# A chunked delta-rule recurrence with state and values stacked on the contraction rows

## Chip, core and metric

The kernel runs on one core of a Trainium2 chip. Its time is the device time of one execution in microseconds (us). The engines work side by side, each with an instruction queue of its own: TensorE (PE for its products, PEld for the weight loads that stand ahead of them), VectorE (DVE), ScalarE (ACT), GpSimd (POOL) and SyncE (SP), which issues most DMAs.

## What is computed

One layer of a decoder trunk on 512 positions of width 2048, all in float32. The input is normalised and multiplied with a wide matrix; part of the columns goes to 16 recurrent heads of width 64, part to a causal pooling branch. Both are gated, joined, multiplied with an output matrix, and a gated embedding and a last normalisation follow. What the change touches is the recurrence of the heads:

```python
def step(S, inp):
    r_t, w_t, k_t, v_t, kk_t, a_t = inp
    sa = jnp.einsum('bhvk,bhk->bhv', S, -kk_t)
    S = (S * w_t[:, :, None, :]
         + sa[..., None] * (kk_t * a_t)[:, :, None, :]
         + v_t[..., None] * k_t[:, :, None, :])
    y_t = jnp.einsum('bhvk,bhk->bhv', S, r_t)
    return S, y_t
```

## The kernel before

The 512 positions are cut into 8 chunks of 64 and the 16 heads into 8 pairs (index `j`), since two heads of width 64 fill 128 partitions. Inside a chunk the recurrence is solved in closed form. With the state S at the chunk's start, the scaled keys and queries (`ar`: the k-side and the r-side; `bk`: the kk-side and the k-side), four masked 64 x 64 products of `bk` with `ar` are needed (`scores`, line L623 masks them on DVE), one of which has to be inverted as a unit triangular matrix (`invert` does its 32 x 32 diagonal blocks on DVE, after a trip through memory by the tensors `nd` and `xd`; the rest of `gather` completes it on TensorE with `pq` and `px`).

Then `recur` goes through the chunks, one head pair at a time. In each chunk there are three hops, each a TensorE product, then a short operation of another engine that the next product needs:

1. `py`: both sides of `ar` times the block-diagonal state `sbd` of the two heads (128 x 128, so one product serves both heads). DVE adds `mv`, the masked product with the values (made for all chunks beforehand by the block `pmv` in `gather`), into `zs` (L787). The first chunk of a head pair has no such hop.
2. `pu`: the inverse `x1` times `zs`. ACT copies the two diagonal blocks into `uv` (L797), where u and v of a chunk lie one above the other.
3. `ps` (`pss` in the code): `bkn`, the transposed `bk`, times `uv`. DVE scales it by the chunk's decay and adds the decayed old state `s0p` (made by POOL), one operation a head (L809); this is the next `sbd`.

After every fourth chunk eight products of half width (`py<-uv,mt` in the profile) add the part of y that comes from inside the chunks, and ACT copies y out (`ysb`).

The hops have nothing to do with each other's engines, so TensorE would stand idle between them. It does not, since the large products of the layer (the input matrix in blocks of 128 columns `zk`, `zr`, `zv`, `zg`, `zb`, and the embedding) are cut into steps and put between the hops. `pump(n)` issues about n of them; they come in threes (`mm3`, L157), because each float32 matrix is split into a high and a low float32r part. What is issued too many is carried over to the next call. `HC` gives the number after each of the three hops, `H1` to `H5`, `HX` those at places in `gather` and around `scores`, and `pump_to` rounds the position after the scores to a unit of `sum(HC)` or to `HC[2]` within it. During this part all TensorE instructions stay in the order of the program. The other engines' instructions are ordered by a scheduler at compile time, with the hand-overs of the hops (`tc.high_priority`) ahead of other work, and the steps of `invert` for the next head pair tied behind the last hand-over (`lead`).

PSUM tiles come from pools: `psM` has three (`m`), `psY` two (`y`), `psS` one, `psA` two for the large products.

Of the kernel before, what the change touches and what calls it, by code (L numbers as in the profile page):

```python
# [9 lines left out]
F32 = mybir.dt.float32  # L10
# [5 lines left out]
P = 128  # L16
T = 512
# [17 lines left out]
def trunk_kernel(ctx: ExitStack, tc: tile.TileContext, x, p, norm_g, w_in, mu, w0, w_up, a0, a_up,  # L35
# [56 lines left out]
    msk = cst.tile([P, 3, C], F32, name="msk")  # L92
    nc.gpsimd.memset(msk, 1.0)
    for h in range(2):
        rows = slice(64 * h, 64 * h + 64)
        for i in range(3):
            keep_if(msk[rows, i, :], [[1, C]], ALU.is_ge, -(i % 2), -1)
# [261 lines left out]
    sbd = [rw.tile([P, P], F32, name=f"sbd{i}") for i in range(2)]  # L359
    zsp = [rw.tile([P, P], F32, name=f"zs{i}") for i in range(2)]  # L360
# [4 lines left out]
    for t_ in sbd + zsp:  # L365
        nc.gpsimd.memset(t_, 0.0)
# [150 lines left out]
    H1, H2, H3, H4, H5, HE = 6, 12, 20, 8, 13, 40  # L517
# [59 lines left out]
    def prepare(j):  # L577
# [3 lines left out]
        if j + 1 < NJ:  # L581
# [3 lines left out]
        ar = rw.tile([P, NCH // 2, 4, C], F32, name=f"ar{j}", tag="ar", bufs=2)  # L585
        bk = rw.tile([P, NCH // 2, 4, C], F32, name=f"bk{j}", tag="bk")
        k4 = kk.rearrange("p (q c t) -> p q c t", c=2, t=C)
        pw4 = pw.rearrange("p (q c) t -> p q c t", c=2)
        i4 = ipw.rearrange("p (q c) t -> p q c t", c=2)
# [4 lines left out]
        nc.vector.tensor_tensor(ar[:, :, 0::3, :], r_.rearrange("p (q c t) -> p q c t", c=2, t=C),  # L594
                                pw4[:, :, :, 1:C + 1], ALU.mult)
        nc.vector.tensor_tensor(bk[:, :, 0::3, :], kp.rearrange("p (q c t) -> p q c t", c=2, t=C), i4, ALU.mult)
        nc.vector.scalar_tensor_tensor(ar[:, :, 1:3, :], k_.rearrange("p (q c t) -> p q c t", c=2, t=C), dp(89, j),
                                       pw4[:, :, :, 0:C], ALU.mult, ALU.mult)
        nc.vector.tensor_tensor(kk, kk, tha, ALU.mult)
        nc.vector.tensor_tensor(bk[:, :, 1:3, :], k4, i4, ALU.mult)  # L600
# [7 lines left out]
    def scores(j):  # L608
        ar, bk, v_ = (st_[j][n_] for n_ in ("ar", "bk", "v_"))
        kph, kpl = st_[j].pop("kp")  # L610

        mt = rw.tile([P, 2, 8, 2, C], F32, name=f"mt{j}", tag="mt", bufs=2)
        pm = [[psM.tile([P, T], F32, name=f"pm{j}_{par}0", tag="m"),
               psY.tile([P, T], F32, name=f"pm{j}_{par}1", tag="y")] for par in range(2)]
        for par in range(2):
            for q in range(4):
                for h in range(2):
                    rows = slice(64 * h, 64 * h + 64)
                    mm(pm[par][h][:, q * P:(q + 1) * P], bk[rows, q, 2 * par:2 * par + 2, :],
                       ar[rows, q, 2 * par:2 * par + 2, :], start=True, stop=True)  # L620
        for par in range(2):
            for h in range(2):
                nc.vector.tensor_tensor(mt[:, par, h::2, :, :],  # L623
                                        pm[par][h].rearrange("p (u a t) -> p u a t", u=4, a=2),
                                        msk[:, par:par + 2, :].unsqueeze(1).to_broadcast([P, 4, 2, C]), ALU.mult)


# [7 lines left out]
        for par in range(2):  # L635
            pb = 64 * (1 - par)
            for b in range(2):
                rows = slice(pb + 32 * b, pb + 32 * b + 32)
                nc.sync.dma_start(out=nd[par, b].rearrange("u r c -> r u c"),
                                  in_=mt[rows, par, :, 1 - par, 32 * b:32 * b + 32])  # L640
# [6 lines left out]
        st_[j].update(mt=mt, nb=nb, bv=bv)  # L647


    def invert(j):  # L650
# [16 lines left out]
        x1 = rw.tile([P, 8, C], F32, name=f"x1{j}", tag="x1", bufs=2)  # L667
        nc.gpsimd.memset(x1, 0.0)
        for par in range(2):
            pb = 64 * (1 - par)  # L670
            for b in range(2):
                nc.sync.dma_start(out=x1[pb + 32 * b:pb + 32 * b + 32, :, 32 * b:32 * b + 32],
                                  in_=xd[par, b].rearrange("u i q c -> (i q) u c"))

# [3 lines left out]
    def gather(j):  # L678
        d = st_[j]
        bk, v_, mt = d.pop("bk"), d.pop("v_"), d["mt"]  # L680
# [4 lines left out]
        uv = rw.tile([P, NCH, P], F32, name=f"uv{j}", tag="uv")  # L685
        ps = psY.tile([P, T], F32, name=f"pv{j}", tag="y")
# [3 lines left out]
        nc.scalar.copy(uv[0:64, 0::2, :], pv[0:64])  # L690
        nc.scalar.copy(uv[64:128, 1::2, :], pv[64:128])


        bkn = rw.tile([P, NCH, P], F32, name=f"bkn{j}", tag="bkn")
        for hf in range(2):
            ps = psM.tile([P, T], F32, name=f"pbk{j}_{hf}", tag="m")
            for i in range(4):
                ch = 4 * hf + i
                tr(ps[:, i * P:(i + 1) * P], bk[:, ch // 2, 2 * (ch % 2):2 * (ch % 2) + 2, :], ident)
            nc.scalar.copy(bkn[:, 4 * hf:4 * hf + 4, :], ps.rearrange("p (c n) -> p c n", n=P))  # L700

        pump(H4)

        ps = psM.tile([P, 8, C], F32, name=f"pmv{j}", tag="m")
        for u in range(8):
            for par in range(2):
                pb, kb = 64 * (1 - par), 64 * par
                h = u % 2
                mm(ps[pb:pb + 64, u, :], mt[kb:kb + 64, par, u, 1 - par, :],
                   uv[kb:kb + 64, 2 * (u // 2) + par, 64 * h:64 * h + 64], start=True, stop=True)  # L710
        mv = rw.tile([P, 4, P], F32, name=f"mv{j}", tag="mv")
        nc.scalar.copy(zsp[0][64:128, :].rearrange("p (h t) -> p h t", h=2), ps[64:128, 0:2, :])
        nc.scalar.copy(mv.rearrange("p q (h t) -> p (q h) t", h=2), ps)

        d.update(uv=uv, bkn=bkn, mv=mv)
# [7 lines left out]
        x1 = d["x1"]  # L723

        def units(fn):
            for u in range(8):
                for par in range(2):
                    fn(u, par, 64 * (1 - par))
# [3 lines left out]
        with tc.issue_after(late[0].ins):  # L732
            for pb in (0, 64):
                yt = nc.vector.transpose(y1[pb:pb + 32], x1[pb:pb + 32, :, 0:32])
# [4 lines left out]
        units(lambda u, par, pb: mm(ps3[pb + 32:pb + 64, u, :],  # L739
                                                  mt[pb:pb + 32, par, u, 1 - par, 32:64],  # L740
                                                  y1[pb:pb + 32, u, :], start=True, stop=True,
                                                  tile_position=(pb, pb + 32)))
        q2t = rw.tile([P, 8, 32], F32, name=f"q2{j}", tag="xw")
        for pb in (0, 64):
# [3 lines left out]
        units(lambda u, par, pb: mm(ps4[pb:pb + 32, u, :], q2t[pb + 32:pb + 64, u, :],  # L748
                                                  x1[pb + 32:pb + 64, u, 32:64], start=True, stop=True,
                                                  tile_position=(pb + 32, pb)))  # L750
        for pb in (0, 64):
            nc.scalar.copy(x1[pb:pb + 32, :, 32:64], ps4[pb:pb + 32])
# [3 lines left out]
    def recur(j, work, between):  # L756
        d = st_.pop(j)
        pw, ar, mt, bv, uv, bkn, mv, x1 = (d[n_] for n_ in ("pw", "ar", "mt", "bv", "uv", "bkn", "mv", "x1"))
# [5 lines left out]
        def step():  # L764
            hop[0] += 1
            if hop[0] > HS:
# [6 lines left out]
        py = None  # L773
        for ch in range(NCH):
            par, q = ch % 2, ch // 2
            pb = 64 * (1 - par)
            cur, nxt = sbd[ch % 2], sbd[(ch + 1) % 2]
            pcc = pw[:, ch, C:C + 1]
            sl = slice((ch % 4) * P, (ch % 4 + 1) * P)
            if ch % 4 == 0:  # L780
                py = psY.tile([P, T], F32, name=f"py{j}_{ch}", tag="y")
            zs = zsp[par]
            if ch > 0:
                mm(py[:, sl], ar[:, q, 2 * par:2 * par + 2, :], cur, start=ch in (1, 4), stop=True,
                                 skip_group_check=True)
                with tc.high_priority(offset=HP):
                    lead[0] = nc.vector.tensor_tensor(zs[pb:pb + 64], py[pb:pb + 64, sl], mv[pb:pb + 64, q, :],  # L787
                                                      ALU.add)
                step()
                pump(HC1)  # L790

            psu = psS.tile([P, T], F32, name=f"pu{j}_{ch}", tag="s")
            mm(psu[:, 0:P], x1[:, 2 * q:2 * q + 2, :], zs, start=True, stop=True)
            for h in range(2):
                hc = slice(64 * h, 64 * h + 64)
                with tc.high_priority(offset=HP):
                    nc.scalar.copy(uv[pb:pb + 64, ch, hc], psu[hc, hc])  # L797
            step()
            pump(HC2)
            if ch < NCH - 1:  # L800
                pss = psS.tile([P, T], F32, name=f"ps{j}_{ch}", tag="s")
                mm(pss[:, 0:P], bkn[:, ch, :], uv[:, ch, :], start=True, stop=True)
                for h in range(2):
                    hc = slice(64 * h, 64 * h + 64)
# [376 lines left out]
```

## Time and profile before

| | |
|---|---|
| median of 3 runs | 1100.12 us (1098.21 to 1101.85) |
| span of the profiled execution | 1095.9 us |
| own time of the profiled execution | not on the page, which gives the span alone |
| busy: PE, PEld, DVE, ACT, POOL | 98%, 80%, 65%, 41%, 7% |
| instructions on TensorE (products) | 6060 |
| granted TensorE clock, mean | 0.998 |

A row of a group has the line, engine, operation, the tile written and those read, the array's rows and columns in use, the shape, the count, then the busy time and the mean of one, then the idle time of the engine ahead of it with what ended it. A timeline row has start and duration in us. PE's durations are modelled and overlap, so what a product costs TensorE is read from the distance of starts.

### The profile page before, as it was taken

Reading aid. Unit: us, or ns where it says so; the run is one execution under the profiler, and the core shown is the slowest. Engines: PE = TensorE matmul, PEld = TensorE weight load, DVE = VectorE, ACT = ScalarE, POOL = GpSimd, SP = SyncE. Lnnn points to the kernel's source line nnn. Section 1 sums busy time; section 2 is a strip of 40 time slices with the busy share of each in tenths; the row PEclk is TensorE's granted clock in tenths of the full one; section 3 lists DMA queues with packets and bytes.
Section 4 is the critical chain, followed back from the end, with each engine's and each line's share of the span. In section 5 each row is a group of like instructions: output and inputs, shape, how many; then the busy total and the mean of one; then the engine's idle time right before and its main releaser. Section 6 shows DMA issues by size and latency. Waiting matters only on the chain.

```text
span 1095.9 us, 17196 instructions
## 1 busy us (share of the span) xinstructions
PE 1070.8 (98%) x6060; PEld 877.6 (80%) x6060; DVE 708.2 (65%) x1835; ACT 448.3 (41%) x917; POOL 76.9 (7%) x180
## 2 busy tenths in 40 slices
PE   5999999999999999999999999999999999999996
PEld 4888878887788888788878788888888888888885
DVE  6687867878688679678886956454433424445366
ACT  7633535345335335353343344543222222233337
POOL 2100110110110110100101101000000000000000
PEclk9999999999999999999999999999999999999999
DMA  7433433332423333333334242775534438455534
GB/s 233 116 96 97 111 92 84 96 100 73 120 82 105 104 92 89 96 82 93 91 94 119 79 138 93 232 233 169 172 124 136 167 99 244 137 189 137 181 106 154
DMA packets 178486, 138.56 MB, mean 126 GB/s; under 512 B 34678, under 2 KB 139743, under 8 KB 178399
## 3 DMA queue, kind: packets, MB, share of 16 engines
q1 hardware_dynamic: 157694, 103.89, 32.1%
q10 hardware_dynamic: 20704, 33.56, 9.8%
q8 instruction: 48, 0.79, 0.3%
q14 instruction: 40, 0.32, 0.1%
HBM read 118.02 MB, written 18.87 MB: 125 GB/s over the span
## 4 chain that ended last, share of the span: by engine, by line
PE 86%; DVE 5%; DMA 4%; ACT 3%; issue 1%; SPq 0%; ACTq 0%; DVEq 0%
PE acc_o L157 16%; PE zb L157 14%; PE acc_g L157 14%; PE zv L157 8%; PE zk L157 7%; PE zg L157 7%; PE zr L157 7%; PE py L157 2%; PE pple L157 2%; PE pm L157 1%; PE pu L157 1%; DMA n<-nd 1%; PE pp L157 1%; DMA raw_g<-in_w_pg_dram 1%; PE ps L157 1%
## 5 line engine op out<-in xcount | busy, mean ns | idle before, releaser
L133 DVE TENSOR_TENSOR wlo_g<-raw_g,whi_g 128x512 fp32r<-128x512 f32 x84 | 57.0, 685 | 79.6 <-ACT whi_g L132 76.5
L157 PE MATMUL zb<-hhi,whi_b 128*128 128x512 f32 x256 | 107.0, 418 | 0.0
L133 DVE TENSOR_TENSOR wlo_o<-raw_o,whi_o 128x512 fp32r<-128x512 f32 x64 | 43.9, 690 | 91.4 <-ACT whi_o L132 91.4
L157 PE MATMUL zb<-hhi,wlo_b 128*128 128x512 f32 x256 | 100.5, 393 | 0.0
L157 PE MATMUL acc_o<-whi_o,ylo 128*128 128x512 f32 x256 | 100.2, 391 | 0.0
L157 PE MATMUL acc_o<-whi_o,yhi 128*128 128x512 f32 x256 | 99.9, 390 | 0.0
L157 PE MATMUL zb<-hlo,whi_b 128*128 128x512 f32 x256 | 99.9, 390 | 0.0
L157 PE MATMUL acc_o<-wlo_o,yhi 128*128 128x512 f32 x256 | 99.8, 390 | 0.0
L132 ACT CAST whi_g<-raw_g 128x512 fp32r<-128x512 f32 x84 | 51.9, 620 | 102.7 <-PE acc_g L157 55.4
L157 PE MATMUL acc_g<-whi_g,x2hi 128*128 128x512 f32 x208 | 81.3, 391 | 0.0
L157 PE MATMUL acc_g<-wlo_g,x2hi 128*128 128x512 f32 x208 | 80.9, 389 | 0.0
L157 PE MATMUL acc_g<-whi_g,x2lo 128*128 128x512 f32 x208 | 80.7, 389 | 0.0
L132 ACT CAST whi_o<-raw_o 128x512 fp32r<-128x512 f32 x64 | 39.9, 623 | 97.0 <-PE acc_o L157 96.7
L816 POOL TENSOR_SCALAR s0p<-sbd,pw 64x64 f32<-64x64 f32 x96 | 56.6, 589 | 322.8 <-DVE sbd L809 255.0
L132 ACT CAST whi_b<-raw_b 128x512 fp32r<-128x512 f32 x64 | 39.7, 621 | 86.5 <-PE zv L157 35.4
L133 DVE TENSOR_TENSOR wlo_b<-raw_b,whi_b 128x512 fp32r<-128x512 f32 x64 | 43.8, 685 | 34.2 <-ACT whi_b L132 32.9
L157 PEld LDWEIGHTS zb<-hhi,wlo_b 128*128 128x128 f32 x256 | 48.0, 188 | 11.1
L661 DVE TENSOR_TENSOR xw<-xw,tm 128x60 f32<-128x60 f32 (+24 forms) x248 | 52.1, 210 | 6.8
L157 PEld LDWEIGHTS acc_o<-wlo_o,yhi 128*128 128x128 f32 x256 | 48.1, 188 | 10.3 <-DVE wlo_o L133 0.4
L157 PEld LDWEIGHTS acc_o<-whi_o,yhi 128*128 128x128 f32 x256 | 48.1, 188 | 9.7
L157 PEld LDWEIGHTS acc_o<-whi_o,ylo 128*128 128x128 f32 x256 | 48.1, 188 | 9.8
L157 PEld LDWEIGHTS zb<-hhi,whi_b 128*128 128x128 f32 x256 | 48.2, 188 | 8.5
(285 smaller groups left out, 2550.0 us busy)
## 6 DMA issues: line engine op xcount, KB each, us to landing
raw_b<-in_w_in_dram SPq DMA_DIRECT2D x64, 256.0 KB
raw_o<-in_w_out_dram SPq DMA_DIRECT2D x64, 256.0 KB
raw_g<-in_w_pg_dram SPq DMA_DIRECT2D x64, 256.0 KB
raw_k<-in_w_in_dram SPq DMA_DIRECT2D x32, 256.0 KB
raw_r<-in_w_in_dram SPq DMA_DIRECT2D x32, 256.0 KB
raw_v<-in_w_in_dram SPq DMA_DIRECT2D x32, 256.0 KB
raw_g<-in_w_in_dram SPq DMA_DIRECT2D x32, 256.0 KB
n<-nd SPq DMA_DIRECT2D x16, 256.0 KB
```

What stands on the lines that cost most here:

```text
L132: nc.scalar.copy(hi, raw)
L133: nc.vector.tensor_tensor(lo, raw, hi.bitcast(F32), ALU.subtract)
L157: i = nc.tensor.matmul(*a, **k)
L661: nc.vector.tensor_tensor(xw[:, 0:n_, s + 1:32], xw[:, 0:n_, s + 1:32], tm[:, 0:n_, 0:w_], ALU.add)
L816: nc.gpsimd.tensor_scalar(s0p[hc, :], nxt[hc, hc], pcn[hc], None, ALU.mult)
```

## The change

State and values are stacked on the 128 contraction rows of one tile `uv` (rows 0 to 63: the state, later u; rows 64 to 127: v). The left sides are stacked to match, per chunk and head: `am` holds the scaled `ar` above the masked matrix for v, `bm` the masked matrix and the transposed `bk` side by side. A product then gives the state's part and the values' part at once, but for one head at a time: py has two products a chunk (one a head), and so has the third hop, now `pt`, which gives the new state and the in-chunk part of y together. Each has 128 weight columns and 64 moving columns. `pu` is one product of the block-diagonal inverse `xi` with a dense `zs` of 64 columns. The block `pmv`, `mv`, `bkn`, `sbd` and the in-chunk y block are gone. zs is copied by ACT, one copy a head; y is a copy by ACT and an addition by DVE. The two sides change places between even and odd head pairs, so that the masks of the next pair go to another third of `am` and `bm`. `scores` works in two halves of four chunks, with `HB` steps between, and masks into `nn`, `am` and `bm`. `ar` has one buffer instead of two.

```diff
-    H1, H2, H3, H4, H5, HE = 6, 12, 20, 8, 13, 40
+    H1, H2, H3, H4, H5, HE = 6, 12, 12, 8, 10, 40
...
-    HC, HT, HX = (6, 9, 9), 130, 13
+    HC, HT, HX, HB = (8, 8, 8), 130, 9, 8
...
+    am = rw.tile([P, NCH, 2, 3, C], F32, name="am")
+    bm = rw.tile([P, NCH, 2, 3, C], F32, name="bm")
+    xi = rw.tile([P, NCH, P], F32, name="xi")
...
+    nc.gpsimd.memset(xi, 0.0)
+    nc.gpsimd.memset(am[64:128, :, :, 1, :], 0.0)
...
+    def scores(j, between=0):
+        par = j % 2
+        nn = rw.tile([P, NCH, C], F32, name=f"nn{j}", tag="nn")
+        for hf in range(2):
+            chs = slice(4 * hf, 4 * hf + 4)
+            pm = [psM.tile([P, T], F32, name=f"pm{j}_{hf}{h}", tag="m") for h in range(2)]
+            for i in range(4):
+                for h in range(2):
+                    rows = slice(64 * h, 64 * h + 64)
+                    mm(pm[h][:, i * P:(i + 1) * P], bk[rows, 4 * hf + i, :, :], ar[rows, 4 * hf + i, :, :],
+                       start=True, stop=True)
             for h in range(2):
...
+                masked(nn[64 * h:64 * h + 64, chs, :], slice(0, 64), 0)
+                masked(am[64:128, chs, h, 2 * par, :], slice(64, 128), 0)
+                masked(bm[:, chs, h, 2 * par, :], slice(0, P), 1)
+            if hf == 0:
+                pump(between)
...
         # gather
+            nc.scalar.copy(bm[:, 4 * hf:4 * hf + 4, :, 1, :], ps.rearrange("p (c h n) -> p c h n", c=4, h=2))
+        for h in range(2):
+            nc.scalar.copy(am[0:64, :, h, j % 2:j % 2 + 2, :], ar[64 * h:64 * h + 64])
...
+        for pb in range(0, P, 32):
+            nc.scalar.copy(xi[pb:pb + 32, :, pb:pb + 32], x1[pb:pb + 32])
...
         # recur, one chunk
-                mm(py[:, sl], ar[:, q, 2 * par:2 * par + 2, :], cur, start=ch in (1, 4), stop=True,
-                    lead[0] = nc.vector.tensor_tensor(zs[pb:pb + 64], py[pb:pb + 64, sl], mv[pb:pb + 64, q, :],
+            for h in range(2):
+                mm(py[:, hcs[h]], am[:, ch, h, par:par + 2, :], uv[:, ch, hcs[h]], start=True, stop=True)
+            for h in range(2):
+                with tc.high_priority(offset=HP):
+                    nc.scalar.copy(zs[hcs[h], :], py[prs[par], hcs[h]])
+            step()
+            pump(HC1)
...
-            mm(psu[:, 0:P], x1[:, 2 * q:2 * q + 2, :], zs, start=True, stop=True)
+            mm(psu, xi[:, ch, :], zs, start=True, stop=True)
...
-                mm(pss[:, 0:P], bkn[:, ch, :], uv[:, ch, :], start=True, stop=True)
+            for h in range(2):
+                mm(pt[:, hcs[h]], bm[:, ch, h, par:par + 2, :], uv[:, ch, hcs[h]], start=True, stop=True)
...
+                            lead[0] = nc.vector.scalar_tensor_tensor(nxt, pt[prs[1 - par], hcs[h]], decay(ch, h),
+                                                                     s0p[:, hcs[h]], ALU.mult, ALU.add)
...
+            if ch % 2 == 1:
+                for i in range(2):
+                    ys = ysb[hcs[i], ch // 2, :]
+                    nc.scalar.copy(ys, yy[prs[1 - par], i, 0, :])
+                    nc.vector.tensor_tensor(ys, ys, yy[prs[par], i, 1, :], ALU.add)
```

More of the change, by code (lines that the diff above doesn't have):

```diff
@@ L90, in trunk_kernel @@
     nc.gpsimd.memset(seg.rearrange("p (c t) -> p c t", t=C)[:, :, 0:1], 0.0)
-    msk = cst.tile([P, 3, C], F32, name="msk")
+    msk = cst.tile([P, 2, C], F32, name="msk")
     nc.gpsimd.memset(msk, 1.0)
@@ L95, in trunk_kernel @@
         rows = slice(64 * h, 64 * h + 64)
-        for i in range(3):
-            keep_if(msk[rows, i, :], [[1, C]], ALU.is_ge, -(i % 2), -1)
+        for i in range(2):
+            keep_if(msk[rows, i, :], [[1, C]], ALU.is_ge, -i, -1)
     i32 = cst.tile([P, 8, 32], F32, name="i32")
@@ L685, in gather @@
         uv = rw.tile([P, NCH, P], F32, name=f"uv{j}", tag="uv")
+        nc.gpsimd.memset(uv[0:64, 0, :], 0.0)
         ps = psY.tile([P, T], F32, name=f"pv{j}", tag="y")
@@ L689, in gather @@
         pv = ps.rearrange("p (t c) -> p t c", c=P)
-        nc.scalar.copy(uv[0:64, 0::2, :], pv[0:64])
-        nc.scalar.copy(uv[64:128, 1::2, :], pv[64:128])
-        bkn = rw.tile([P, NCH, P], F32, name=f"bkn{j}", tag="bkn")
+        for i in range(2):
+            nc.scalar.copy(uv[64:128, i::2, :], pv[64 * i:64 * i + 64])
         for hf in range(2):
@@ L697, in gather @@
             for i in range(4):
-                ch = 4 * hf + i
-                tr(ps[:, i * P:(i + 1) * P], bk[:, ch // 2, 2 * (ch % 2):2 * (ch % 2) + 2, :], ident)
-            nc.scalar.copy(bkn[:, 4 * hf:4 * hf + 4, :], ps.rearrange("p (c n) -> p c n", n=P))
+                tr(ps[:, i * P:(i + 1) * P], bk[:, 4 * hf + i, :, :], ident)
+            nc.scalar.copy(bm[:, 4 * hf:4 * hf + 4, :, 1, :], ps.rearrange("p (c h n) -> p c h n", c=4, h=2))
+        for h in range(2):
+            nc.scalar.copy(am[0:64, :, h, j % 2:j % 2 + 2, :], ar[64 * h:64 * h + 64])
         pump(H4)
[L704 to L715, printed above, removed]
+        d.update(uv=uv)
         if j + 1 < NJ:
@@ L757, in recur, with decay @@
         d = st_.pop(j)
-        pw, ar, mt, bv, uv, bkn, mv, x1 = (d[n_] for n_ in ("pw", "ar", "mt", "bv", "uv", "bkn", "mv", "x1"))
+        pw, bv, uv = (d[n_] for n_ in ("pw", "bv", "uv"))
+        par = j % 2
+        prs = [slice(64 * i, 64 * i + 64) for i in range(2)]
+        def decay(ch, h):
+            return pw[prs[h], ch, C:C + 1]
         hop = [0]
@@ L765, in step @@
             hop[0] += 1
-            if hop[0] > HS:
+            if hop[0] > HS and lead[0] is not None:
                 with tc.issue_after(lead[0].ins):
```

141 lines of the change are left out of this document (46 added, 95 removed).

## Prediction

> **What bounds the kernel now.** I read the page first, then the waits of TensorE and of its weight loader, then the TensorE groups with shapes kept apart, then the timelines of PE and PEld around each kind of insert, last the DVE and ACT groups and the DVE timeline.
>
> ```profile
> span 1095.9 us, 17196 instructions
> ...
> PE 1070.8 (98%) x6060; PEld 877.6 (80%) x6060; DVE 708.2 (65%) x1835; ACT 448.3 (41%) x917; POOL 76.9 (7%) x180
> ...
> PEld py L157 <- DVE sbd L809: 5.2, 9, 1.4
> ...
> PEld pu L157 <- DVE zs L787: 2.9, 6, 0.9
> ```
>
> TensorE is busy 98% of the span, so a change is worth what it adds to or takes from TensorE's own queue, plus what TensorE waits for the recurrence. What the hops of the recurrence make it wait shows at the weight loader: 5.2 us for the state, 2.9 us for zs, 8.1 us together. No improvement of the hand-over between engines can give more than that. The sum below is made on the span of 1095.9 us; the median of the runs, 1100.12, lies 4.2 us above it, and I carry those 4.2 us (what lies around the span, and the spread of runs) over unchanged.
>
> What the changed lines issue on TensorE:
>
> ```profile
> L157 PE MATMUL pu<-zs,x 128*128 128x128 f32 x128 | 25.1, 278 | 0.8 <-DVE zs L787 0.4
> L157 PE MATMUL py<-sbd,ar 128*128 128x128 f32 x112 | 22.4, 281 | 1.8 <-DVE sbd L809 1.6
> L157 PE MATMUL ps<-uv,bkn 128*128 128x128 f32 x112 | 21.4, 273 | 0.0
> L157 PE MATMUL pm<-ar,bk 64*128 64x128 f32 x256 | 16.4, 278 | 0.0
> ...
> L157 PE MATMUL py<-uv,mt 128*64 128x64 f32 x256 | 11.0, 228 | 0.0
> ...
> L157 PE MATMUL pmv<-uv,mt 64*64 64x64 f32 x256 | 9.2, 221 | 0.0
> ```
>
> The means overlap each other and are no prices. The counts matter: 128 for pu are 8 head pairs x 8 chunks x 2, so an f32 product is two instructions, each with a weight load of its own. Prices come from starts in the timeline: from the last filler before an insert to the second one after it, less two undisturbed steps.
>
> ```profile
> 281.05 0.40 PE L157 MATMUL zg<-hhi,whi_g 128*128 128x512 f32 x1
> ...
> 283.56 0.39 PE L157 MATMUL zg<-hhi,wlo_g 128*128 128x512 f32 x1
> 283.88 2.06 PE L157 MATMUL pm<-ar,bk 64*128 64x128 f32 x32
> ...
> 286.20 0.39 PE L157 MATMUL pbo<-kpl,blk 128*128 128x512 f32 x1
> ...
> 287.59 0.39 PE L157 MATMUL zg<-hhi,wlo_g 128*128 128x512 f32 x1
> 287.82 0.38 PE L157 MATMUL py<-sbd,ar 128*128 128x128 f32 x2
> ...
> 288.27 0.39 PE L157 MATMUL zg<-hlo,whi_g 128*128 128x512 f32 x1
> ...
> 262.78 0.39 PE L157 MATMUL zb<-hhi,wlo_b 128*128 128x512 f32 x1
> 263.10 1.15 PE L157 MATMUL pmv<-uv,mt 64*64 64x64 f32 x32
> ...
> 264.51 0.39 PE L157 MATMUL pss<-kql,blk 128*128 128x512 f32 x1
> ...
> 305.10 0.39 PE L157 MATMUL zk<-hhi,wlo_k 128*128 128x512 f32 x1
> 305.33 0.38 PE L157 MATMUL ps<-uv,bkn 128*128 128x128 f32 x2
> 305.64 0.69 PE L157 MATMUL py<-uv,mt 128*64 128x64 f32 x16
> ...
> 306.59 0.39 PE L157 MATMUL zr<-hlo,whi_r 128*128 128x512 f32 x1
> ```
>
> A filler step is 0.228 us (281.05 to 283.56 is 11 steps). One 128-column product (py) costs 288.27 - 287.59 - 0.456 = 0.22 us. The pmv block costs 264.51 - 262.78 - 0.456 = 1.27. ps with the in-chunk block behind it costs 1.03, so the block alone 0.81. The pm block costs 286.20 - 283.56 - 0.456 = 2.18.
>
> **Products of the recurrence.** Before, a head pair has 7 py, 8 pu and 7 ps: 22 x 0.22 = 4.84; two in-chunk blocks, 1.62; one pmv block, 1.27. Sum 7.73 us. After, both blocks are gone, but each chunk has py for each of two heads, one pu, and pt for each of two heads: 5 products, 40 a head pair, all with 128-column weights and 64 moving columns instead of 128. No such shape is in the trace. The question is what sets 0.22: the moving columns or the weight loads.
>
> ```profile
> 271.45 0.58 PEld L157 LDWEIGHTS pq<-y,mt 32*32 32x32 f32 x32 [0.35 <-issue]
> 272.08 0.19 PEld L157 LDWEIGHTS zb<-hhi,whi_b 128*128 128x128 f32 x1
> 272.19 0.19 PEld L157 LDWEIGHTS zb<-hlo,whi_b 128*128 128x128 f32 x1
> ...
> 283.88 1.86 PEld L157 LDWEIGHTS pm<-ar,bk 64*128 64x128 f32 x32 [0.35 <-issue]
> ```
>
> Behind the pq block, whose products are only 32 columns wide, one 128-column load starts 0.11 us after the other (272.08, 272.19) with no wide product between them. So 0.11 is the load's own time, and two loads are the 0.22 of a product. Halving the moving columns saves nothing. I take 0.22 for a 64-column product: 40 x 0.22 = 8.80, which is +1.07 a head pair, **+8.6 us** over eight. The other end is a price that goes with moving columns, 0.11: 40 x 0.11 = 4.40, -3.33 a head pair, -26.6 us. The pair of loads is the nearest row and excludes it nearly; I keep it as a rival. The Trainium skill ("TensorE: Matmul & The Clock Gate", section "LDWEIGHTS (loading the stationary operand)") speaks against this change too: load time goes with weight columns alone, and 128 / 1.2 GHz is 107 ns, with which the 0.11 agrees. Its section "Back-to-back issue gap" puts 64 columns at about 60 cycles and 128 at 134; by that alone the sum would be near the -26.6.
>
> **Scores in two halves.** Still 16 pm products, now 8 + 8 with 6 or 9 fillers between (HB). The loader row has 32 loads in 1.86 us, the last one 0.19 long, so a pair of loads (two heads side by side) takes 1.67 / 15.5 = 0.107 and 16 pairs 1.71. The remaining 2.18 - 1.71 = 0.47 is entering and leaving the half-height form, now paid twice; for head pair 0 nothing stands between the halves. 7 x 0.47 = **+3.3 us** (ends 0 and twice that). The Trainium skill ("TensorEngine Tiling (Array Packing)") says that changing the tiling mode drains TensorE; the 0.35 of issue ahead of the pm loads agrees.
>
> The two halves take four psM tiles out of three. The second half's last tile waits until DVE has masked the first half's first one, with three operations of 256 elements each instead of one of 512.
>
> ```profile
> L623 DVE TENSOR_TENSOR mt<-pm,msk 128x512 f32<-128x512 f32 x32 | 19.9, 682 | 0.9 <-PE pm L157 0.8
> L787 DVE TENSOR_TENSOR zs<-py,mv 64x128 f32<-64x128 f32 x56 | 16.1, 287 | 17.7 <-PE py L157 16.8
> ...
> L133 DVE TENSOR_TENSOR wlo_g<-raw_g,whi_g 128x512 fp32r<-128x512 f32 x84 | 57.0, 685 | 79.6 <-ACT whi_g L132 76.5 <-DMA raw_g<-in_w_pg_dram 2.1 <-DMA pler<-pled 0.7
> ...
> L797 ACT COPY uv<-pu 64x64 f32<-64x64 f32 x128 | 26.4, 206 | 47.5 <-PE pu L157 46.5
> ```
>
> Between 0.287 (128 elements) and 0.682 (512) a 256-element one is about 0.42 (estimate): 1.26 us, some 0.4 to start, and a weight split of 0.685 that may stand ahead, against 6 or 9 fillers (1.37 or 2.05). A wait of 0 to 1.0 us; I take 0.3 for each of seven, **+2 us** (ends 0 and 7).
>
> **Hand-overs.** zs moves from one DVE addition (0.287) to two ACT copies (2 x 0.206). The filler behind py grows: HC goes from 6, 9, 9 to 8, 8, 8, and as fillers come in threes, 8, 8, 8 is dealt as 9, 9, 6 or, where the alignment after the scores lands on a half unit, 9, 6, 9. Counting through the job list gives 9, 9, 6 in head pairs 0, 2, 4, 6, 7 and 9, 6, 9 in 1, 3, 5. The total is 255 fillers a head pair before and after, so none is left over. The 2.9 us of waits for zs should go: 2.05 us cover two copies, as they cover uv's now. Without that cover a hop would cost some 0.4 us. The shorter step is then the state hand-over (two DVE operations) in five head pairs: 1.37 us where there were 2.05.
>
> ```profile
> 297.94 0.38 PE L157 MATMUL ps<-uv,bkn 128*128 128x128 f32 x2
> ...
> 300.98 0.29 DVE L809 SCALAR_TENSOR_TENSOR sbd<-ps,pw,s0p 64x64 f32<-64x64 f32 x1
> ...
> 301.33 0.49 PE L157 MATMUL py<-sbd,ar 128*128 128x128 f32 x2 [0.92 <-DVE sbd L809]
> ...
> 305.82 0.28 DVE L809 SCALAR_TENSOR_TENSOR sbd<-ps,pw,s0p 64x64 f32<-64x64 f32 x1 [0.85 <-PE ps L157]
> ...
> 306.73 0.29 DVE L809 SCALAR_TENSOR_TENSOR sbd<-ps,pw,s0p 64x64 f32<-64x64 f32 x1
> ```
>
> In the chunk at 305.33 DVE was waiting, put a weight split between its two operations, and ended 1.58 us after the second ps instruction (305.44 to 307.02): with 6 fillers nearly in time. In the chunk at 297.94 it came late, since the first step of the inverse held DVE until its rows came back from memory, and ended 3.22 us after: a wait of 0.92 under 9 fillers, 1.6 under 6. One such chunk a head pair, plus a few tenths on the others, is 1.9 us x 5 = 9.5; three pairs keep their share of 5.2, 2.0. So 11.5 replace 5.2, and 2.9 go: **+3.4 us** (ends -8.1, all waits gone, and +13).
>
> **Covered, at nothing.** The second PSUM reads for y (ACT copy and DVE add, 8 a head pair) and the bm copies have nobody behind them until the chunk pair ends. The two 1024-element ACT copies of ar, which prepare's writes now also wait for since ar has one buffer, and the four xi copies lie beside the 24 to 27 fillers of gather (over 5 us). The memsets of am and xi are on POOL, 7% busy. x1's memset there goes. The nd, n, xd and x1 transfers keep number and bytes on SP's queue. If gather's cover failed, each head pair would pay about 1 us.
>
> **Sum.** 1100.1 + 8.6 + 3.3 + 2 + 3.4 = 1117.4; I say 1117.
>
> **Rivals.** (a) Faster, by one mechanism: a product is paid by its moving columns. -26.6 + 3.3 + 2 + 3.4 = -18, 1082. For it: the work in columns does fall. Against it: the two loads 0.11 apart. It decides once a 64-column product costs less than 0.156 us: then the 320 products give back the sum's 17.3 and 3.3 more, 0.064 each. 8 in 100. (b) The waits go away: 1100.1 + 8.6 + 3.3 - 8.1 = 1104. For it: DVE loses one of two hand-overs a chunk; against it: five pairs get a shorter cover at the other. 17 in 100. (c) DVE becomes the bound in the recurrence: every one of the 56 chunk ends late by 0.5 us, 28 in place of 11.5, and 7 at the scores: 1139. For it: DVE gets about 12 x 0.42 + 8 x 0.287 and loses 4 x 0.682 + 7 x 0.287, +2.6 us a head pair, and the state step has lost cover; against it: most chunks have DVE in time. 12 in 100. (d) It doesn't do what it says, loads partly hide under neighbours, and the terms cancel: 1100, 7 in 100. The forecast, 1110 to 1126, has 56.
>
> The measurement can tell about 0.3%, 3.3 us. Faster: (a), 0.08. Same: (d) and a part of (b), 0.10. Slower: 0.82. The range leaves out (a), (d) and the top of (c): 1102 to 1131.
>
> **What would show it.** In the after profile: 64-column am, bm and xi products, 640 instructions, stepping 0.11 us, with four of them costing 0.44 between fillers; pm in two blocks of about 1.3 us each; waits of TensorE on uv from DVE up in head pairs 0, 2, 4, 6, 7 and none on zs; the granted clock as before. A step of 0.06 between two such products would make the forecast wrong on the fast side; long waits of pm on DVE, on the slow side.

## The result and the profile after

The changed kernel takes 1163.91 us (median of 4 runs, 1163.03 to 1164.89); the kernel before took 1099.68 beside it (4 runs). The ratio is 1.0583, 95% interval 1.0564 to 1.0602: slower, by almost four times what I forecast (+17) and far outside the range. The profiled run of the changed kernel has a span of 1161.5 us, 65.6 more than before. Everything below is accounted on spans.

The page of the changed kernel, its span, the first row of busy time and the row of granted clock over 40 slices:

```profile
span 1161.5 us, 17064 instructions
...
PE 1101.4 (95%) x5836; PEld 905.3 (78%) x5836; DVE 731.8 (63%) x1907; ACT 501.5 (43%) x1109; POOL 64.9 (6%) x176
...
PEclk9989999999998998998999999999999999999999
```

TensorE's share of busy time fell from 98% to 95%, and its clock, whole in nearly every slice before (mean 0.998), has holes (mean 0.98). It waits for something, then. The waits of TensorE and of its weight loader in the changed kernel (engine, tile and line waited for; us in total, times, longest):

```profile
PE pyt L161 <- DVE ysb L835: 26.3, 9, 5.9
...
PE yy L157 <- DVE uv L800: 6.3, 7, 2.1
...
PE pbo L157 <- DVE bm L626: 2.8, 4, 0.9
PE pm L157 <- DVE bm L626: 2.0, 1, 2.0
...
PEld yy L157 <- DVE uv L800: 10.1, 10, 2.5
```

The first row is the largest part of the loss. pyt is the transpose of the normalized y, at the head of finish, and ysb at L835 is VectorE's scaling of y ahead of it. Before, this wait was not in the list at all. The waits that I had argued about, for uv and bm, are the smaller rows.

The place itself, once in each kernel. First VectorE in the changed kernel after head pair 3 has ended, from the statistics of y to their last use (start, duration, line, operation, tile):

```profile
446.13 0.35 DVE L826 BATCH_NORM_STATS2 st<-ysb 128x6 f32<-128x64 f32 x2
...
447.06 0.17 DVE L831 TENSOR_SCALAR ve<-mvr 128x8 f32<-128x8 f32 x1
...
448.00 1.23 DVE L535 TENSOR_TENSOR_SCAN sig<-seg,sig 128x512 f32<-128x512 f32 x1
449.14 0.14 DVE L150 TENSOR_TENSOR nt<-nt,rs 128x8 f32<-128x8 f32 x1
449.20 0.54 DVE L593 TENSOR_SCALAR kp<-tha,dprm 128x512 f32<-128x512 f32 x1
449.66 0.17 DVE L151 SCALAR_TENSOR_TENSOR rs<-nt,rs 128x8 f32<-128x8 f32 x1
449.78 0.69 DVE L594 TENSOR_TENSOR kp<-kp,sk 128x512 f32<-128x512 f32 x1
...
453.93 0.17 DVE L151 SCALAR_TENSOR_TENSOR rs<-nt,rs 128x8 f32<-128x8 f32 x1
454.01 3.35 DVE L573 RECIPROCAL kk<-kk 128x512 f32<-128x512 f32 x1
457.27 0.63 DVE L133 TENSOR_TENSOR wlo_g<-raw_g,whi_g 128x512 fp32r<-128x512 f32 x1
457.82 1.86 DVE L835 TENSOR_SCALAR ysb<-ysb,mvr,rs 128x64 f32<-128x64 f32 x8
```

The kernel before, same place of the same head pair:

```profile
409.72 0.17 DVE L850 TENSOR_SCALAR ve<-mvr 128x8 f32<-128x8 f32 x1
...
414.79 0.16 DVE L151 SCALAR_TENSOR_TENSOR rs<-nt,rs 128x8 f32<-128x8 f32 x1
...
415.21 1.87 DVE L854 TENSOR_SCALAR ysb<-ysb,mvr,rs 128x64 f32<-128x64 f32 x8
...
419.72 3.35 DVE L572 RECIPROCAL kk<-kk 128x512 f32<-128x512 f32 x1
```

The small operations on 128x8 are the inverse square root for y, a dozen that depend on one another. In the changed kernel one operation of the next head pair's decay, key and prepare steps, mostly of 512 elements, stands between nearly every two of them, and then the reciprocal of the next key, 3.35 us, ahead of the scaling. Before, other operations stood between some of them too, but the scaling came ahead of the reciprocal. Against the last y product, the scaling of this head pair ends 6.7 us later than before: the small operations begin 1.4 us later, take 7.0 us from first to last where they took 5.2, and the reciprocal with the weight split behind it puts 3.7 us ahead of the scaling where 0.3 stood. TensorE beside it, in the changed kernel, and the granted clock in four stretches:

```profile
452.39 0.39 PE L157 MATMUL zb<-hhi,wlo_b 128*128 128x512 f32 x1
458.49 1.72 PE L161 MATMUL pyt<-ident,ysb 128*128 128x128 f32 x4 [5.71 <-DVE ysb L835]
...
460.87 0.63 PE L157 MATMUL zb<-hhi,wlo_b 128*128 128x512 f32 x1
461.29 0.63 PE L157 MATMUL zb<-hhi,whi_b 128*128 128x512 f32 x1
461.72 0.63 PE L157 MATMUL zb<-hlo,whi_b 128*128 128x512 f32 x1
...
462.93 0.39 PE L157 MATMUL zb<-hlo,whi_b 128*128 128x512 f32 x1
463.16 0.40 PE L157 MATMUL zb<-hhi,wlo_b 128*128 128x512 f32 x1
```

```profile
450.00:457.00 7.00, 2.78 (x13) 1.97 (x11) 6.91 (x14) 4.91 (x12) 0.00 (x0) 0.93 0.16 47
457.00:459.90 2.90, 1.41 (x5) 0.71 (x5) 2.90 (x11) 0.00 (x0) 0.00 (x0) 0.50 0.24 65
459.90:464.00 4.10, 4.10 (x42) 3.11 (x42) 3.98 (x7) 1.40 (x2) 0.00 (x0) 0.64 0.08 22
464.00:470.00 6.00, 6.00 (x68) 4.82 (x63) 3.56 (x7) 3.69 (x9) 0.40 (x1) 1.00 0.31 98
```

In the first fence TensorE stands 5.71 us; then the fillers step 0.43 us (461.29 to 461.72) instead of 0.23 (462.93 to 463.16). In the second, columns are the stretch, its length, the busy time of PE, PEld, DVE, ACT and POOL, then the granted clock: 0.50 at the end of the wait, 0.64 behind it, 1.00 four microseconds later. So a wait is paid twice, as standing and as slow fillers.

I summed this over the whole trace in the prediction's way: from the last filler before an insert to the second one after it, less two undisturbed steps; and, for the clock, each filler step over 0.40 us less 0.229.

| us | products and hops | pm | pq and px | pyt | slow fillers | span |
|---|---|---|---|---|---|---|
| before | 69.6 | 17.5 | 13.2 | 3.6 | 0.3 | 1095.9 |
| after | 80.8 | 27.0 | 14.9 | 39.0 | 10.2 | 1161.5 |
| difference | +11.2 | +9.5 | +1.7 | +35.4 | +9.9 | +65.6 |

The columns add up to 67.7, or 2.1 more than the span grew; that difference is in inserts not listed and in the method's error. Two thirds, 45 us, are the y transposes and the slow fillers, for which the prediction had nothing. Of the 10.2 us of slow fillers, 6.9 stand behind waits of pyt, 2.1 behind the wait of pm in head pair 0, and 1.2 behind a wait for the state in head pair 3.

### The profile page after: what moved, and what is told of

The parts are those of the page before. It is cut to its first block, busy times and chain, and to the rows that moved or that the text cites. A ratio compares the mean times of both kernels' runs of the same rounds, so it can differ in the third digit from the quotient of the medians.

```text
span 1161.5 us, 17064 instructions
## 1 busy us (share of the span) xinstructions
PE 1101.4 (95%) x5836; PEld 905.3 (78%) x5836; DVE 731.8 (63%) x1907; ACT 501.5 (43%) x1109; POOL 64.9 (6%) x176
## 4 chain that ended last, share of the span: by engine, by line
PE 63%; DVE 7%; DMA 3%; ACT 1%; issue 1%; SPq 0%; ACTq 0%; DVEq 0%
PE acc_o L157 15%; PE acc_g L157 15%; PE zb L157 10%; PE zv L157 4%; PE zr L157 4%; PE zg L157 4%; PE yy L157 3%; PE zk L157 2%; PE pple L157 2%; DMA n<-nd 2%; DVE kk L573 1%; PE pp L157 1%; PE pm L157 1%; PE px L983 1%; DMA raw_v<-in_w_in_dram 1%
## 5 line engine op out<-in xcount | busy, mean ns | idle before, releaser
L157 PE MATMUL zb<-hhi,whi_b 128*128 128x512 f32 x256 | 110.0, 430 | 0.0
L805 POOL TENSOR_SCALAR s0p<-uv,pw 64x64 f32<-64x64 f32 x96 | 50.9, 530 | 363.2 <-DVE uv L800 291.0
L132 ACT CAST whi_b<-raw_b 128x512 fp32r<-128x512 f32 x64 | 39.7, 620 | 43.8 <-PE zv L157 10.3
L157 PEld LDWEIGHTS zb<-hhi,wlo_b 128*128 128x128 f32 x256 | 49.2, 192 | 11.5
L157 PEld LDWEIGHTS zb<-hlo,whi_b 128*128 128x128 f32 x256 | 49.8, 195 | 8.1
```

The lines of the kernel that those rows point to most:

```text
L132: nc.scalar.copy(hi, raw)
L157: i = nc.tensor.matmul(*a, **k)
L805: nc.gpsimd.tensor_scalar(s0p[:, hcs[h]], uv[0:64, ch + 1, hcs[h]], decay(ch + 1, h), None, ALU.mult)
```

## The experiments

Their question was first why pyt waits, then why taking the wait away gives back less than its size, and last what the change costs when nothing is late. Each time stands beside the kernel before on the same chip (medians 1097.6 to 1098.2); the ratio is to that.

**E1: the reciprocal behind the y scaling.** One thing of VectorE's order is put back.

```diff
-            with tc.issue_after(yt.ins):
+            with tc.issue_after((scaled_y[0] or yt).ins):   # the last y scaling
                 scale_key(j + 1)
```

> The changed kernel with one order forced on DVE: the reciprocal of the next head pair's key norm (3.35 us) is tied behind the last scaling of y, instead of behind the transposes of the inverse. Theory A (DVE does the reciprocal, and a weight split, ahead of the scaling that the y transposes wait for): in the five head pairs where the reciprocal stood ahead, the wait of 5.7 us falls by 3.8 us, and with shorter idle times the granted clock comes back; 1164 becomes about 1137, and the wait left on the y transposes is about 1 us a pair. Theory B (y is simply finished too late for the place of its transposes, whatever the order, and the clock follows): no less than 1155, waits of 4 us a pair stay.

Measured: 1150.62, ratio 1.0477 (1.0459 to 1.0496). The pyt inserts fall from 39.0 to 28.7, the slow fillers from 10.2 to 7.2. The reciprocal is part of the cause, and less than I expected: in the head pairs where it had stood ahead of the scaling (four, not five: 0, 2, 3 and 4), the scaling still ends some 13 us after the last y product, since the other operations of prepare stay in between.

**E2: finish later, VectorE's order as changed.** TensorE gets the cover back, not the order.

```diff
         pump(H5)
-        if pending:
-            pending.pop()()
         pump(HX)
 ...
         pump(H1)                      # end of gather
+        if pending:
+            pending.pop()()
```

> The changed kernel with the transposes of y (finish) moved behind the whole of gather, 21 fillers and the pq and px blocks later (about 6.4 us); the DVE order is left to the scheduler. Both theories of the wait on y expect the waits of the y transposes gone in head pairs 0 to 6 (7 x 4.8 us) and the clock near 1.0 (some 8 us): about 1122. The rival that most of the 64 us is in the hops themselves (products, hand-overs) expects no less than 1150.

Measured: 1134.73, ratio 1.0335 (1.0318 to 1.0353). The pyt inserts fall to 11.1 and the slow fillers to 3.4: 34.7 us less. The span falls by 26.0 only, to a time some 13 us above the expected one: pm rises to 30.0, pq and px to 19.4, and the products to 82.4. With the cover put right most of the wait goes; a part of it comes back elsewhere.

**E4: the kernel before, its first y scaling behind the next reciprocal.** The order is broken where everything else is as before.

```diff
-        nc.vector.reciprocal(kk, kk)
+        rcp = nc.vector.reciprocal(kk, kk)
+        if y_sc:
+            tc.add_manual_dep(y_sc[0].ins, rcp.ins.name, ...)   # order on VectorE only
```

> The kernel before with one order reversed on DVE: the first of the eight scalings of y behind the reciprocal of the next pair. The theory expects the wait to appear in the old kernel: the scaling ends 8.8 to 10.4 us after the last y product there, TensorE is free at 11.2 to 12.9, and some 4 to 5 us more on DVE make 2 to 4 us of wait in each of seven pairs: 1098 becomes 1112 to 1125. If DVE's order is not what counts: 1098.

Measured: 1133.20, ratio 1.0321 (1.0306 to 1.0337), more than either side expected. The waits of TensorE, and VectorE at head pair 3, in this kernel:

```profile
PE pyt L161 <- DVE ysb L859: 23.3, 6, 4.3
```

```profile
438.34 3.35 DVE L573 RECIPROCAL kk<-kk 128x512 f32<-128x512 f32 x1
441.61 0.63 DVE L133 TENSOR_TENSOR wlo_g<-raw_g,whi_g 128x512 fp32r<-128x512 f32 x1
442.16 0.30 DVE L859 TENSOR_SCALAR ysb<-ysb,mvr,rs 128x64 f32<-128x64 f32 x1
```

One scaling of 0.30 us was moved behind the reciprocal and what stands ahead of it, while the other seven stayed in their place. In six head pairs the last scaling so ends 5 to 7 us later. The pyt inserts go from 3.6 to 31.0 and the slow fillers from 0.3 to 8.8: 36 us, and the span rises by 35.0. So this order alone, without one of the new products, makes a loss of the kind that the change shows.

**E3: the kernel before with fewer fillers around finish.** The change cuts H5 (ahead of finish) and HX (behind it); these counts alone are tried.

```diff
-    H1, H2, H3, H4, H5, HE = 6, 12, 20, 8, 13, 40
-    HC, HT, HX = (6, 9, 9), 130, 13
+    H1, H2, H3, H4, H5, HE = 6, 12, 20, 8, 10, 40
+    HC, HT, HX = (6, 9, 9), 130, 9
```

> The kernel before with the changed kernel's filler counts ahead of and behind the y transposes (H5 10, HX 9 in place of 13 and 13), nothing else. If the counts alone make the wait: 5 us a pair as in the changed kernel, 1130 or more. If the old order on DVE keeps its margin of 0.9 to 2.8 us: within 4 us of 1098, since the fillers left out are run later.

Measured: 1096.77 (10 runs), ratio 0.9994 (0.9985 to 1.0004), the pyt inserts 3.5. No change in the time (pm inserts that are 2.7 us higher stand against products and hops that are 3.2 lower): three fillers ahead of pyt are 0.7 us, and the old order has 1 to 3 us in hand. TensorE came to pyt 11.2 to 12.9 us after the last y product, with the scaling done after 8.8 to 10.4. After, TensorE comes at 8.4 to 9.2 in head pairs 0 to 4 and 6 (10.5 in head pair 5), and the scaling ends at 15.4 to 16.1 in head pairs 0, 2, 3 and 4. Both sides moved, TensorE by 2 to 3 us and VectorE by 5 to 7.

**E8: everything of prepare behind the y scaling.** E1 with the nine VectorE operations of prepare tied as well.

```diff
+        with tc.issue_after((scaled_y[0] or late[0]).ins):
             nc.vector.tensor_scalar(kp, tha, dp(33, j), dp(41, j), ALU.mult, ALU.add)
             ...                       # to the last of the nine
```

> The changed kernel with DVE's order at the end of a head pair set in full: the reciprocal and all nine DVE operations of prepare stand behind the last scaling of y; TensorE's order is as in the changed kernel. Theory (y ends late because other large DVE operations stand between its statistics and its scaling): with prepare's operations gone from between, about 5 us come off the 13.2 us that the scaling's end took after the last y product when only the reciprocal was moved; TensorE is free 8.5 to 9.2 us after that product, so the wait of the y transposes is 0 to 1 us and the time falls to about 1130. Rival (the window before the transposes was cut too far for any order): waits of 3 us a pair stay, 1145 or more.

Measured: 1138.90, ratio 1.0388 (1.0356 to 1.0419), between the two. The waits of TensorE in this kernel:

```profile
PE pm L157 <- DVE bk L602: 6.8, 4, 3.5
...
PE yy L157 <- DVE uv L802: 6.7, 7, 2.2
PE pbo L157 <- DVE bm L628: 4.7, 6, 1.5
...
PE pyt L161 <- DVE ysb L837: 1.6, 3, 1.1
```

The wait of pyt is gone (26.3 to 1.6; its inserts 7.8), with the slow fillers halved (4.7). What was ahead of it on VectorE is now late for the scores: pm waits for bk, and the pm inserts are 39.7. VectorE has too little slack at this place for both, so an order gives to one what it takes from the other. The edit leaves the second PSUM reads for y as they are, so these alone don't make the wait of pyt.

**E5: scores in one piece.** The 16 pm products go back into one block, in four PSUM tiles, as before; the fillers of HB follow it.

```diff
-            pm = [psM.tile([P, T], F32, name=f"pm{j}_{hf}{h}", tag="m") for h in range(2)]
+        pms = [[psM.tile(...), psY.tile(...)], [psM.tile(...), psS.tile(...)]]
 ...
-            if hf == 0:
-                pump(between)
+        pump(between)                 # once, behind the masks
```

> The changed kernel with scores in one piece: all 16 products in a row into four PSUM tiles of three pools, then the masks, and the HB fillers behind. By the after trace the pm blocks and the waits in and behind them cost 27 us against 17.5 before, and the second half of head pair 0 waits and lets the clock fall: in one piece 2.2 us a pair again, 10 us less plus 2 of clock, 1152. If the halves cost nothing: 1164.

Measured: 1157.67, ratio 1.0551 (1.0530 to 1.0572), whose interval touches that of the change. The pm inserts are 17.7, as before. The time lies between the two that were expected. Of the 9.3 us that the pm inserts give, 6.4 reach the span, while the pyt wait stands as it was and the slow fillers, at 10.8, do not fall.

**E6 and E9: both together.** E6 is E2 with E5, E9 is E8 with E5.

> Both edits, the late y transposes and the scores in one piece. If the three terms (waits on y with the clock they cost, the halves of the scores, the products) account for the 64 us, what is left over the kernel before is the products alone, 11 us by the distance of starts (81 us against 70), plus the last head pair's wait: 1112 to 1115. If they don't add up, something unnamed is left: over 1120.

> The same with the scores in one piece. If what is left is products and the waits of the hops: 1120. Where moving the y transposes and the scores together gave no more than moving the transposes alone, the saving of the scores came back as a wait for the state; if that is DVE standing at the first step of the inverse, it shows here too, and the time is 1128.

Measured: E6 1135.14, ratio 1.0336 (1.0316 to 1.0357): no better than E2 alone, and some 20 us above the expectation. E9 1133.18, ratio 1.0331 (1.0298 to 1.0365), 5 to 13 us above the two figures expected. Something unnamed was left in both. In E6 pm falls to 18.2, and the products and hops rise from 82.4 to 91.8, against a floor of 72 (128 inserts of 0.451 and 64 of 0.225). The waits of TensorE and then of VectorE in E6:

```profile
PE yy L157 <- DVE uv L802: 13.9, 7, 4.4
```

```profile
DVE tm L663 <- DMA n<-nd: 34.3, 8, 6.8
```

The second row is the first step of the next pair's inverse: VectorE stands there until its rows have come back from memory, 17.3 us in the kernel before, 22.2 in the change, 34.3 here. The first two, in the kernel before and in the changed one:

```profile
DVE tm L657 <- DMA n<-nd: 17.3, 8, 3.8
```

```profile
DVE tm L661 <- DMA n<-nd: 22.2, 8, 4.1
```

The number that places this step, HS, counts hops. The change left it at 5, but its first chunk has three hops where the old one had two, so its inverse begins one hop earlier than before; no run takes back that hop alone. The state's operations are queued behind the step. That gave the last question.

**E10 and E11: the inverse begun later.** E9 and E6 with the first step of the inverse three hops, that is one chunk, later.

```diff
-    HS, HN = 5, 2
+    HS, HN = 8, 2
```

> The changed kernel with e9's two edits (y scalings ahead of the prepare operations on VectorE, scores in one piece), and the next pair's inverse started three half-steps later (HS 8 for 5, so its first VectorE step, which stands until its rows come back from memory, falls a chunk later). The e9 kernel spent 73.0 us on the yy inserts where 128 x 0.451 = 57.7 is their floor, and 11.9 us of it are waits for uv from VectorE. Theory (the remaining state waits come from VectorE standing at the inverse's first step, with wlo splits and prepare queued behind): yy sum falls to 64 to 67, waits of TensorE for uv to about 5, time 1133 - 7 = 1126. Rival (the state hand-over is simply too long for the 6 or 9 fillers, or the backlog of VectorE after finish is what is late): yy sum stays at 71 to 75, time 1131 to 1136. Second rival: the inverse, begun later, is late for its last steps, pq and px rise by 3 us or more, time 1133 to 1138.

> The changed kernel with e6's two edits (finish moved behind gather, scores in one piece) and HS 8 for 5. The e6 kernel waited 13.9 us for uv from VectorE, and VectorE stood 34.3 us at the inverse's first step waiting for its rows from memory (17.3 in the kernel before). Theory (standing there is what makes the state late): waits for uv fall to about 6, VectorE's standing to below 20, time 1135 - 8 = 1127. Rival (VectorE's backlog behind the finish is what is late, and standing is only idle time): waits for uv and time unchanged within 2 us, 1133 to 1137.

Measured: E10 1122.42, ratio 1.0227 (1.0210 to 1.0245); E11 1115.11, ratio 1.0155 (1.0134 to 1.0176). Both fall by more than the theory said, 10.8 and 20.0 us. The weight loader's waits in E6 and, second, in E11, and VectorE's standing in E11:

```profile
PEld yy L157 <- DVE uv L802: 17.9, 11, 4.8
```

```profile
PEld yy L157 <- DVE uv L802: 0.4, 2, 0.2
```

```profile
DVE tm L663 <- DMA n<-nd: 6.8, 1, 6.8
```

The one standing left is that of head pair 0, ahead of the recurrence. Products and hops are 72.6, at their floor. The price is at the inverse's end, as the second rival of E10 had it: pq and px together rise from 19.2 to 19.9 in E11, and from 14.1 to 19.5 in E10.

**E12: E11 with the scores in halves again.**

> The changed kernel with the finish behind gather and HS 8 for 5, but with its scores in two halves as the change has them: against e11 (1115.11, ratio 1.0155) only the halves differ. Theory (the halves cost what the trace of the change shows between the fillers, pm inserts 27.0 us against 17.7 whole, once nothing else is late): pm inserts 25 to 27 us, time 1115 + 8 = 1123, ratio 1.021 to 1.024. Rival (the halves' wait for VectorE is given back, since what VectorE is given later it is not behind with elsewhere): ratio 1.014 to 1.018, with pq, px or yy inserts lower than e11's by what pm is higher. The forecast's own size for the halves was 5.3 us (3.3 for the second entry and 2 of wait): ratio 1.020.

Measured: 1129.84 (1125.47 to 1132.27), ratio 1.0299 (1.0277 to 1.0321). That is 14.7 us above E11, more than every size that I had named; the profiled run is the fastest of the five, and there the span is 9.4 above that of E11's profiled run, the slowest of E11's four. Its pm inserts are 30.2 against 18.2, with pq and px, products and pyt equal within 0.6. In the other four runs the granted clock is lower (0.988 to 0.992 against 0.994), so the rest lies probably in slow fillers; no trace of those runs was read. The rival, that the halves' cost is given back, is out.

**E7: the kernel before with its inverse begun later.** One number, in the kernel before.

```diff
-    HS, HN = 5, 2
+    HS, HN = 7, 2
```

> The kernel before with its inverse started two half-steps later (HS 7 for 5), nothing else. The kernel before waits 5.2 us for the state at the weight loader, most of it in the chunk in which VectorE stands at the inverse's first step. Theory (that standing is the cause there too): the 5.2 us fall to 2 to 3 and the time by 2 to 3 us, 1095 to 1096, ratio 0.997 to 0.998. Rival: the standing moves one chunk on and makes that chunk late instead: ratio 0.999 to 1.001. A second rival: the inverse ends late and pq or px wait: ratio above 1.001.

Measured: 1092.59 (6 runs, 1091.89 to 1093.41), ratio 0.9955 (0.9941 to 0.9969). The weight loader's waits and VectorE's standing in this kernel:

```profile
PEld py L157 <- DVE sbd L809: 1.0, 2, 0.7
```

```profile
DVE tm L657 <- DMA n<-nd: 3.9, 1, 3.9
```

The 5.2 us of waits for the state fall to 1.0, and seven of eight standings are gone. This is the fastest version here, below both kernels; the gain is larger than the 2 to 3 us expected.

## Why the prediction was wrong

The direction was right, the size was not. The forecast had four terms and one cover; they stand so.

**Products of the recurrence, forecast +8.6: right.** A product of 64 moving columns costs what one of 128 cost. In the changed kernel, two products of y and one of U between fillers:

```profile
467.58 0.39 PE L157 MATMUL zb<-hhi,wlo_b 128*128 128x512 f32 x1
467.81 0.55 PE L157 MATMUL yy<-uv,am 128*128 128x64 f32 x4
...
468.49 0.39 PE L157 MATMUL zg<-hlo,whi_g 128*128 128x512 f32 x1
...
470.11 0.40 PE L157 MATMUL zg<-hhi,wlo_g 128*128 128x512 f32 x1
470.34 0.33 PE L157 MATMUL pu<-zs,xi 128*128 128x64 f32 x2
...
470.79 0.39 PE L157 MATMUL zg<-hlo,whi_g 128*128 128x512 f32 x1
```

468.49 - 467.58 - 0.456 = 0.45 for four instructions, 470.79 - 470.11 - 0.456 = 0.22 for two. Over the trace the medians are 0.451 and 0.226, and the floors of all inserts are 72.2 after and 62.9 before: +9.3. Rival (a), payment by moving columns, is out. In the Trainium skill ("TensorE: Matmul & The Clock Gate"), the table of the section "Back-to-back issue gap" has about 60 cycles for 64 columns and 134 for 128; the recurrence's products, at 0.113 us an instruction with either, do not follow it. The rule on weight loads in its section "LDWEIGHTS (loading the stationary operand)", 107 ns for 128 weight columns, agrees with them better.

**Hand-overs, forecast +3.4: the size nearly right, in part by luck.** Products and hops rose by 11.2, of which 9.3 are floor: +1.9. The waits for zs went, as forecast, and the loader waits 10.1 us for the state where I had 11.5. But I had put 9.5 of these on the five head pairs with fewer fillers behind the third hop (0, 2, 4, 6, 7). These wait 4.2, head pair 4 not at all, while the three that kept 9 fillers (1, 3, 5) wait 5.9 where I had 2.0. The longest is in head pair 3:

```profile
410.74 0.52 PEld L157 LDWEIGHTS yy<-uv,am 128*128 128x128 f32 x4 [2.51 <-DVE uv L800]
```

So the fillers taken away do not say where the waits fall. The other reason that I gave, VectorE held at the first step of the inverse, was a real cause, as E7, E10 and E11 show; I had not seen that it could be taken away with one number, in the kernel before too. Rival (c) took VectorE for the bound at the hops, with 28 us of waits for the state there; all waits of the hops together, by the inserts (80.8 less their floor of 72.2), were 8.6.

**Scores in two halves, +3.3, and the wait for psM, +2: the mechanism right, the sizes too small, 9.5 against 5.3.** The second entry was nearly right, at 3.3: 14 inserts of 1.291 against 7 of 2.184 is +2.8. The waits of seven pairs were 2.9, near the 2 that I took. What I left out is head pair 0, of which I wrote that nothing stands between its halves, and to which I gave no price: the second half follows at once, waits for the masks (the row of pm waiting 2.0 for bm), and the inserts cost 6.0 instead of 2.2, with 2.1 us of slow fillers behind them. In E12, with its inverse and finish later, the waits of the seven pairs are larger still, 7.1.

**"Covered, at nothing": the step that failed.** I wrote that the second PSUM reads for y have nobody behind them until the chunk pair ends, and costed the edits around y at nothing. Behind the last chunk pair stands a whole chain: statistics, a dozen small operations, eight scalings, then pyt on TensorE. Its cover before was what TensorE did between the last y product and finish, and the margin was only 1 to 3 us (1.9 in head pair 3, 11.2 against 9.4). The change takes the pmv block (1.27) and three to six fillers (0.7 to 1.4) out of just this stretch in nearly every head pair, and I had followed the fillers only in their sum, 255 before and after. And I did not ask in which order VectorE would be given the chain among prepare's operations: it is another one than before, with the reciprocal ahead in four head pairs. The second reads themselves are the smaller part: in head pairs 0 to 5 the small operations begin 0.4 to 1.4 us later behind the last y product. E4 shows that an order of this kind costs 35 us by itself, E2 and E8 that putting back either cover or order takes most of the wait away. Why the scheduler chose this order was not tried; E1 shows that the reciprocal alone is not all of it.

**"The granted clock as before": wrong, and a consequence.** The slow fillers are 9.9 us, and they come and go with the waits (10.2 after, 8.8 in E4, 4.7 in E8, none in E7).

Had the cover held, would 1117 have been right? E2, which puts back the cover alone, is at 1134.7. E12 comes nearest to the case asked for: the change as a whole, with finish and inverse so placed that the state waits nowhere and pyt little, at 1129.8. So no. Its span is 27.9 above the one before: products and hops +2.6, where I had 12.0 together; pm +12.7, where I had 5.3; and pq and px +6.1, pyt +7.2 and slow fillers +1.6, where I had nothing (their sum is 30.2). With whole scores (E11) it is 1115.1, which is near 1117 only by what cancels, 17.5 above the kernel before and 22.5 above E7. No version run here makes the new form pay.

## What to carry to other kernels

When a change shortens what an engine does between a producer's end and the consumer, write down for that place, not for the sum, when the consumer arrives and when the chain of small dependent operations ends on the engine that feeds it; a margin of 2 us in the old trace is not a cover. One operation of 0.30 us, tied behind a long one on VectorE, cost about 6 us in each of six head pairs (E4). Where VectorE has little slack, moving its work moves the wait unless something is taken out of its way, such as a step that stands on a transfer. Look for such a standing step first: delaying it by two or three hops was worth 5 us in the old kernel (E7) and 20 in E11 against E6.

## What the runs showed of the hardware

After TensorE had waited 2.9 to 5.9 us for the y scaling in the change, E1 and E4 (14 times), the fillers always stepped about 0.43 us instead of 0.228 for 4 to 11 of them, which cost 0.9 to 2.3 us each time. Other waits of 1 to 3.5 us were followed by it in some places and not in others: in E8 one of 1.09 us was (1.4 us lost), one of 2.2 us was not. At the pm of the same head pair, one of 3.45 us in E8 was followed by five slow fillers, and one of 3.43 us in E9 by none. The Trainium skill ("TensorE: Matmul & The Clock Gate", section "What's actually happening") has half clock after an idle window of about 3.4 us. The waits of 4.0 to 5.9 us and the granted clock of 0.50 agree; that waits of a third of that length can do it too, the page does not lead one to expect. What decides between 1 and 3.5 us stays open.
